# The recurrence's output products in two phases: all with states, then all with values

## The chip, the cores and the metric

The kernel runs on one core of a Trainium2 chip. What counts is the device time of one launch in microseconds, from the first to the last instruction of the program. Three runs of the kernel before the change gave 1718.55, 1724.16 and 1728.1 us, so the median is 1724.16 us.

The core has a matrix engine (TensorE, in the rows PE, and PEld for its loading of weights), a vector engine (VectorE, DVE), a scalar engine (ScalarE, ACT), a general one (GpSimd, POOL) and a queue that issues transfers (SyncE, SP). Each runs its own list of instructions in order and waits on the others through semaphores.

## The reference

Two blocks of a network work on 256 tokens of `x`, 1024 wide; the first block also has 256 tokens of `ctx`. Each block has two layers of a mixer and a gated feed-forward product. The change lies in the first block's mixer, which joins a Fourier mix, attention and a gated recurrence of four heads (64 keys, 64 values) that runs forward and backward over chunks of 64 tokens:

```python
def step(s, inp):                      # one chunk; s is the state, 64 x 64
    kc, vc, lf = inp[0], inp[1], inp[2]
    cum = jnp.cumsum(lf, axis=2)
    last = cum[:, :, -1:, :]
    s_new = jnp.exp(last[:, :, 0, :])[..., None] * s + \
        jnp.einsum('bhsd,bhse->bhde', kc * jnp.exp(last - cum), vc)
    if not with_out:
        return s_new, None
    qc = inp[3]
    o_inter = jnp.einsum('bhtd,bhde->bhte', qc * jnp.exp(cum), s)
    ...
    att = jnp.einsum('bhtd,bhsd,bhtsd->bhts', qc, kc, decay)
    return s_new, o_inter + jnp.einsum('bhts,bhse->bhte', att, vc)
```

The output of a chunk is thus a product of queries with the state before it (`o_inter`), for each direction, plus a product of weights inside the chunk with its values. In layer 0 both sequences (`ctx` is sequence 0, `x` is sequence 1) have an output, in layer 1 only `x`; `ctx` then only hands its state on.

## The kernel before

Large products (`gemm`, L176 to L178) take weights that arrive in float32, are split by ScalarE (L169) and VectorE (L170) into two halves, and enter TensorE as three products of the halves. The parts of a mixer are queued in the order of the table `STEPS`: `z0` and `z1` project gates, values and queries for two heads each, `h00` is the recurrence of sequence 0 and heads pair 0, `k`, `q`, `u`, `g` are further projections, `a` the attention. All engines' lists are laid down by a scheduler that mixes these parts, so small products of the recurrence stand between large ones in TensorE's list.

One call `h_(seq, fd)` treats a pair of heads, with the features of both heads on the 128 partitions. It has four parts:

- `hgrn_gates` turns gates and queries on TensorE (L1064), takes sigmoids on ScalarE, and makes the tile `xy` of keys and queries.
- `hgrn_levels` computes the weights inside chunks in six levels and a diagonal. In each level ScalarE copies halves of `xy` into `kq` (tile `hkm`, L1123 and L1124), TensorE makes eight products of 64 x 64 into two banks of the group `tr` (L1098), VectorE copies both banks under a mask (L1108) and scales `xy` in place for the next level.
- `hgrn_states` multiplies keys with values (L1163), folds the states of chunks on VectorE (L1178), and ScalarE copies them into `hsb` (L1190).
- `hgrn_out` makes the outputs in bank `o`. Tokens of even chunks fall on partitions 0 to 63, those of odd chunks on 64 to 127. For each chunk and head it issues up to two products of queries (128 rows, 64 columns) with states (L1204), and then one of weights with values (64 rows, 64 columns; L1206).

A float32 product is recorded as two passes, each with its own load of weights: 176 passes of L1204 are 88 products, 96 of L1206 are 48. There are six calls with outputs: four in layer 0 and two in layer 1. A call of sequence 1 has 16 products with states, one of sequence 0 has 12, and each has 8 with values.

Of the kernel before, what the change touches and what calls it, by code (L numbers as in the profile page):

```python
# [20 lines left out]
P = 128  # L21
# [8 lines left out]
# the order in which the parts of a first block's mixer are queued, for each layer  # L30
# [64 lines left out]
class Net:  # L95
    def __init__(self, ctx, tc, A, out, taps=None, stop=None):
# [15 lines left out]
        self.flip = 0  # L112
        self.late_bufs, self.late_rate = 8, 0.6
# [8 lines left out]
    # -- helpers ---------------------------------------------------------  # L122
# [36 lines left out]
    def copy(self, out, in_):  # L159
        """Copy on ScalarE and VectorE in turn."""  # L160
# [6 lines left out]
    def split(self, hi, lo, src):  # L167
        """src = hi + lo, both float32r."""
# [15 lines left out]
    # -- constants -------------------------------------------------------  # L184
    def setup(self, fp):
# [7 lines left out]
        # layer 0's c and c_ctx, and its modulation's biases, as columns  # L193
# [12 lines left out]
        # c and c_ctx as the first two of 32 columns, the others zero  # L206
# [5 lines left out]
        # sums of the rows 0, 32, 64, 96 and of 1, 33, 65, 97  # L212
# [7 lines left out]
    def setup_late(self):  # L220
        """The second block's condition and gains, as columns."""
# [30 lines left out]
    def ada_first(self, pool, k0, kn, mods):  # L252
        """k-tiles k0..k0+kn of layer 0's first scales and shifts, for c and c_ctx."""
# [22 lines left out]
    def ada_cols(self, row, j, k0, kn, dests):  # L276
        """The sums of rows as columns, k-tiles k0..k0+kn, with their biases."""
# [124 lines left out]
    def mod_tiles(self, name, gates=True):  # L402
        """Columns sh_a, sc_a, sh_f, sc_f and gate rows a, f of one modulation."""
# [13 lines left out]
    def fold_gain(self, mods, i, gi):  # L417
        """(1 + sc) *= gain, on columns."""
# [13 lines left out]
    def row_rstd(self, x, junk):  # L432
        """(mean of squares + eps) ** -0.5 of each row of x [P, D]."""
# [12 lines left out]
    def norm_t(self, pool, res, pair, sh, sc, hT, col0):  # L446
        """Two token tiles of res, normalised, modulated and turned: hT[:, :, col0 : col0 + 256]."""
# [30 lines left out]
    def norm_row(self, res, tt, sh, sc, hT, gain=None):  # L478
        """One token tile of res, normalised, modulated and turned; the turning is left pending.
        With gain, a norm with that gain goes before, and is kept in res."""  # L480
# [17 lines left out]
        else:  # L498
            # of x * gain / rms(x), in terms of x * gain
# [54 lines left out]
    def norm_first(self, pool, srcs, sh, sc, hT):  # L554
        """Two sequences from DRAM, normalised and turned while their modulations come."""
# [58 lines left out]
    def more_weights(self, name=None):  # L614
        """Open, or close, a second pool that every other chunk of weights goes to."""
# [19 lines left out]
    def gemm_steps(self, xT, ktiles, w, w0, n0, nw, toks, widths=None, after=None, ahead=0, halved=False, early=False):  # L635
        """gemm, with pauses between chunks of weights but the last ones."""
# [101 lines left out]
    def out_proj(self, xT, nk, w, w0, toks, targets, gates, after=None):  # L738
        """targets += gates * (x @ w), for the tokens at toks; after: called as each is done."""
# [43 lines left out]
    def ffn(self, pool, hT, wg, wu, wd, toks, targets, gates, parts, after=None):  # L783
        """after: called when a pair of token tiles is done."""
# [480 lines left out]
    def mix1(self, hp, pool, l, hT, start=None, late=None):  # L1265
# [81 lines left out]
        def H_(seq):  # L1347
# [4 lines left out]
            for both in levels:  # L1352
                pass
# [480 lines left out]
```

## Time and profile before

| | before |
|---|---|
| timed runs, us | 1718.55, 1724.16, 1728.1 (median 1724.16) |
| profiled execution, span in us | 1727.1 |
| TensorE busy | 1659.6 us, 96% of the span |
| VectorE, ScalarE busy | 1223.2 us (71%), 850.5 us (49%) |
| TensorE share of the chain that ended last | 72% |
| mean granted clock of TensorE | 0.989 of full speed |

The page gives the profiled execution's span and no separate time around it; it stands 2.9 us above the median and inside the three runs. Busy times of TensorE are pipelined: an instruction's duration has the tail of its pass in it, so how fast passes follow each other is read from their starts in the timeline.

### The profile page before, as it was taken

The numbers are of one execution on the slowest core, as the hardware profiler recorded it, in microseconds if no ns is written. First come the engines' busy times: TensorE is split into PE (matmuls) and PEld (weight loads), VectorE is DVE, ScalarE is ACT, GpSimd is POOL, SyncE is SP. The second block draws the span as 40 slices with busy tenths as digits, with TensorE's granted clock in tenths as the row PEclk, the third lists the DMA queues.
The fourth block names the chain that finished last, engine by engine and source line by source line (L and its number), as shares of the span: only waits on it lengthen the run. The fifth ranks groups of instructions, "written<-read, shape, count | busy, mean of one in ns | idle before, by whom it ended". The sixth has DMA issues, their size and how long they took to land.

```text
span 1727.1 us, 25168 instructions
## 1 busy us (share of the span) xinstructions
PE 1659.6 (96%) x9299; PEld 1328.1 (77%) x9299; DVE 1223.2 (71%) x2042; ACT 850.5 (49%) x1661; POOL 43.6 (3%) x53
## 2 busy tenths in 40 slices
PE   8999999999999999998999999999999999999998
PEld 5677766877777877787767878777777888778886
DVE  4556774886978887777768887787776567575555
ACT  4434483543333334554655445676544456464443
POOL 0000100000000000101000000000000000000000
PEclk9998999999999999999999999999999999999999
DMA  9550405465678886531348897543876543265653
GB/s 326 174 172 25 156 13 194 149 199 166 202 246 280 269 264 210 164 108 50 107 159 284 286 318 250 160 123 121 257 241 194 179 146 90 74 180 166 197 168 118
DMA packets 169473, 310.34 MB, mean 180 GB/s; under 512 B 12163, under 2 KB 72819, under 8 KB 169350
## 3 DMA queue, kind: packets, MB, share of 16 engines
q1 hardware_dynamic: 168966, 308.17, 55.7%
q8 instruction: 73, 1.20, 0.3%
q10 hardware_dynamic: 384, 0.56, 0.1%
q14 instruction: 50, 0.41, 0.1%
HBM read 307.64 MB, written 1.05 MB: 179 GB/s over the span
## 4 chain that ended last, share of the span: by engine, by line
PE 72%; DVE 10%; DMA 8%; ACT 5%; issue 3%; POOL 1%; SPq 1%; ACTq 0%; POOLq 0%; DVEq 0%
PE bank L178 19%; PE bank L177 19%; PE bank L176 18%; DVE wlo L170 3%; ACT whi L169 2%; PE bank L935 2%; PE bank L862 2%; DMA raw<-w_down 1%; DVE acc L357 1%; DMA adaw<-ada_w 1%; PE bank L1204 1%; DMA raw<-ffn_w_in 1%; PE bank L1431 1%; DMA raw<-ffn_w_out 1%; PE bank L320 1%
## 5 line engine op out<-in xcount | busy, mean ns | idle before, releaser
L169 ACT CAST whi<-raw 128x1024 fp32r<-128x1024 f32 (+2 forms) x420 | 400.8, 958 | 521.2 <-PE bank L178 238.1
L170 DVE TENSOR_TENSOR wlo<-raw,whi 128x1024 fp32r<-128x1024 f32 (+2 forms) x420 | 463.5, 1109 | 251.9 <-ACT whi L169 244.2
L176 PE MATMUL bank<-whi,hh 128*128 128x512 f32 (+2 forms) x1200 | 443.9, 373 | 9.3 <-ACT hh L169 5.8
L177 PE MATMUL bank<-wlo,hh 128*128 128x512 f32 (+2 forms) x1200 | 443.4, 370 | 2.7 <-DVE wlo L170 2.7
L178 PE MATMUL bank<-whi,hl 128*128 128x512 f32 (+2 forms) x1200 | 443.1, 371 | 0.2 <-DVE hl L170 0.2
L176 PEld LDWEIGHTS bank<-whi,hh 128*128 128x128 f32 x1200 | 227.8, 191 | 47.5 <-ACT hh L169 7.8
L178 PEld LDWEIGHTS bank<-whi,hl 128*128 128x128 f32 x1200 | 228.8, 191 | 36.0 <-DVE hl L170 3.6
L177 PEld LDWEIGHTS bank<-wlo,hh 128*128 128x128 f32 x1200 | 228.8, 191 | 35.8 <-DVE wlo L170 4.9
L357 DVE SCALAR_TENSOR_TENSOR acc<-adaw,cs,acc 128x1024 f32<-128x1024 f32 x154 | 196.1, 1280 | 20.1 <-DMA adaw<-ada_w 10.9
L177 PE MATMUL bank<-wlo,acth 128*128 128x512 f32 x440 | 175.0, 398 | 0.5 <-DVE wlo L170 0.5
L176 PE MATMUL bank<-whi,acth 128*128 128x512 f32 x440 | 175.3, 399 | 0.0
L178 PE MATMUL bank<-whi,actl 128*128 128x512 f32 x440 | 173.9, 395 | 0.0
L176 PE MATMUL bank<-hh,whi 128*128 128x512 f32 (+1 forms) x376 | 143.3, 382 | 0.0
L177 PE MATMUL bank<-hl,whi 128*128 128x512 f32 (+1 forms) x376 | 143.0, 381 | 0.0
L178 PE MATMUL bank<-hh,wlo 128*128 128x512 f32 (+1 forms) x376 | 142.5, 382 | 0.2 <-DVE wlo L170 0.2
L177 PEld LDWEIGHTS bank<-wlo,acth 128*128 128x128 f32 x440 | 83.5, 190 | 18.8 <-DVE wlo L170 1.1
L178 PEld LDWEIGHTS bank<-whi,actl 128*128 128x128 f32 x440 | 83.5, 190 | 18.6
L176 PEld LDWEIGHTS bank<-whi,acth 128*128 128x128 f32 x440 | 83.4, 189 | 18.5
L178 PEld LDWEIGHTS bank<-hh,wlo 128*128 128x128 f32 x376 | 70.1, 188 | 15.2 <-DVE wlo L170 0.4
L177 PEld LDWEIGHTS bank<-hl,whi 128*128 128x128 f32 x376 | 70.6, 188 | 14.5
L176 PEld LDWEIGHTS bank<-hh,whi 128*128 128x128 f32 x376 | 70.5, 188 | 14.4
L735 DVE TENSOR_TENSOR rtmp<-bank,gate 128x512 f32<-128x512 f32 x68 | 46.5, 686 | 31.5 <-PE bank L178 31.5
(295 smaller groups left out, 1904.3 us busy)
## 6 DMA issues: line engine op xcount, KB each, us to landing
adaw<-ada_w SPq DMA_DIRECT2D x96, 512.0 KB
adaw<-w_ada SPq DMA_DIRECT2D x80, 512.0 KB
raw<-ffn_w_in SPq DMA_DIRECT2D x64, 512.0 KB
raw<-w_down SPq DMA_DIRECT2D x46, 512.0 KB
raw<-ffn_w_out SPq DMA_DIRECT2D x40, 512.0 KB
raw<-w_gate SPq DMA_DIRECT2D x32, 512.0 KB
raw<-w_up SPq DMA_DIRECT2D x32, 512.0 KB
raw<-w_in SPq DMA_DIRECT2D x56, 256.0 KB
```

The source lines that it names most:

```text
L169: a = self.nc.scalar.copy(hi, src)
L170: b = self.nc.vector.tensor_sub(lo, src, hi.bitcast(F32))
L176: mm(out, lh, rh, start=start, stop=False)
L177: mm(out, lh, rl, start=False, stop=False)
L178: mm(out, ll, rh, start=False, stop=stop)
L320: nc.tensor.matmul(ps[h][32 * g : 32 * g + 32], self.cs32[:, k0 + g], raws[g][:, h * 512 : h * 512 + 512], start=k0 == 0, stop=k0 > 0,)
L357: nc.vector.scalar_tensor_tensor(acc, raw, s, acc, op0=ALU.mult, op1=ALU.add)
L735: nc.vector.tensor_mul(tmp[:, :nw], ps[:, :nw], gate[:, n0 : n0 + nw])
L862: self.nc.tensor.transpose(ps[:, i * P : i * P + P], ps_in[:, i * P : i * P + P], self.ident)
L935: self.nc.tensor.matmul(o[e * 64 : e * 64 + 64], v, pt[:, e::2, i], start=i == 0, stop=i == len(vs) - 1)
L1204: mm(dst, q, sb[:, d, i, hp], start=n == 0, stop=False)
L1431: nc.tensor.matmul(dst, q, ksT[:, i, kv, :nk], start=i == 0, stop=i == 1)
```

## The change

`hgrn_out` no longer finishes one chunk and head after the other. First it issues all products with states, so that chunks, and with them the halves of the output's partitions, alternate from product to product; then all products with values. Only the first product into each half of the bank has the flag that starts an accumulation. In the same edit the parts before it are written for a list of head pairs (`nf` of them); the table `STEPS` still calls each with one pair, so `nf` is 1 everywhere. With one pair this remains different:

- queries are turned after both halves of the gates and into a bank of their own, and copied once instead of twice; one VectorE product with a broadcast operand becomes two;
- a level's eight products alternate between the two heads, so both banks are filled at once, and the second ScalarE copy of a level becomes two;
- the products of keys with values run over chunks innermost.

```diff
     def hgrn_out(...):
-        for c in range(4):
-            r = slice((c % 2) * 64, (c % 2) * 64 + 64)
-            steps = [(d, c if d == 0 else 3 - c) for d in range(2)]
-            steps = [(d, i) for d, i in steps if 4 * seq + i]
-            for hp in range(2):
-                o0 = ((c // 2) * 4 + 2 * fd + hp) * 64
-                dst = o[r, o0 : o0 + 64]
-                for n, (d, i) in enumerate(steps):
-                    q = xy[:, 2 - d, c * 64 : c * 64 + 64]
-                    mm(dst, q, sb[:, d, i, hp], start=n == 0, stop=False)
-                v = zn[fd][r, 2 * seq + c // 2, 256 + hp * 64 : 256 + hp * 64 + 64]
-                mm(dst, att[r, hp, c // 2], v, start=False, stop=True)
+        mm, nf = self.nc.tensor.matmul, len(fds)
+        col = lambda c, fd, hp: ((c // 2) * 4 + 2 * fd + hp) * 64
+        cleared = [False, False]
+        for j, fd in enumerate(fds):
+            for d in range(2):
+                for hp in range(2):
+                    for c in range(4):
+                        i = c if d == 0 else 3 - c
+                        if 4 * seq + i == 0:
+                            continue
+                        r, o0 = slice((c % 2) * 64, (c % 2) * 64 + 64), col(c, fd, hp)
+                        q = xy[:, (2 - d) * nf + j, c * 64 : c * 64 + 64]
+                        mm(
+                            o[r, o0 : o0 + 64], q, sbs[fd][:, d, i, hp],
+                            start=not cleared[c % 2], stop=False,
+                        )
+                        cleared[c % 2] = True
+        for j, fd in enumerate(fds):
+            for hp in range(2):
+                for c in range(4):
+                    r, o0 = slice((c % 2) * 64, (c % 2) * 64 + 64), col(c, fd, hp)
+                    v = zn[fd][r, 2 * seq + c // 2, 256 + hp * 64 : 256 + hp * 64 + 64]
+                    mm(
+                        o[r, o0 : o0 + 64], att[r, hp, 2 * j + c // 2], v,
+                        start=False, stop=j == nf - 1 and hp == 1 and c > 1,
+                    )
...
     def hgrn_gates(...):
-            for j, c in enumerate((0, 1, 3) if with_q else (0, 1)):
-                nc.tensor.transpose(
-                    ps[:, j * P : j * P + P], z[:, c * P : c * P + P], self.ident
-                )
...
-                nc.vector.tensor_copy(q[:, 0, ts], ps[:, 256:384])
+        if with_q:
+            ps = self.tr_bank()
...
+            nc.vector.tensor_copy(
+                q[:, :nf], ps[:, : nf * 256].rearrange("p (j t) -> p j t", t=256)
+            )
...
     def hgrn_levels(...):
-            for hp in range(2):
-                ps = self.tr_bank()[:, :128].rearrange("p (g t) -> p g t", g=2)
-                hs = slice(hp * 64, hp * 64 + 64)
+            banks = [
+                self.tr_bank()[:, : nf * 128].rearrange("p (g t) -> p g t", t=64) for _ in range(2)
+            ]
+            for j in range(nf):
                 for c in range(4):
...
+                    for hp in range(2):
...
-                nc.scalar.copy(kv[:, ::-1, :, 1], half(xy)[:, 2:4, :, 1])
+                for s in range(2):
+                    nc.scalar.copy(
+                        kv[:, (1 - s) * nf : (2 - s) * nf, :, 1],
+                        half(xy)[:, (2 + s) * nf : (3 + s) * nf, :, 1],
+                    )
```

What moves on the engines is seen at three places. The first is TensorE's list in layer 0 where the outputs of sequence 1, head pair 0, are made; `hsb` marks products with states, `hatt` those with values, L176 to L178 large products around them. Before:

```order
L177 MATMUL bank_381_2005<-wlo_2083,hh_112 128x512
L1204 MATMUL bank_314_1603<-hsb_581,hxy_1606 64x64 x2
L1206 MATMUL bank_314_1603<-zn_586,hatt_1625 64x64
L178 MATMUL bank_381_2005<-whi_2082,hl_113 128x512
L1204 MATMUL bank_314_1603<-hsb_581,hxy_1606 64x64 x2
L1206 MATMUL bank_314_1603<-zn_586,hatt_1625 64x64
```

The last two rows then repeat until eight such pairs are through. Now, at the same place (the lines have moved by one for L176 to L178; L1249 is the product with states, L1259 that with values, L1081 the turning of queries of the next call):

```order
L177 MATMUL bank_385_2033<-whi_2110,hh_112 128x512
L1249 MATMUL bank_316_1617<-hsb_581,hxy_1620 64x64 x4
L178 MATMUL bank_385_2033<-wlo_2111,hh_112 128x512
L1249 MATMUL bank_316_1617<-hsb_581,hxy_1620 64x64 x12
L1259 MATMUL bank_316_1617<-zn_586,hatt_1640 64x64 x8
L1081 MATMUL bank_355_1837<-ident_73,zn_798 128x128 x2
```

The sixteen changes between the two shapes of a call have become two, and a large product that stood between the parts stands between the first four and the last twelve products with states.

The second place is one level of the next call in TensorE's list (`hkm` is the copy of keys and queries). Before:

```order
L177 MATMUL bank_382_2006<-wlo_2071,hh_112 128x512
L1098 MATMUL bank_357_1839<-hkm_1836 64x64 x4
L1098 MATMUL bank_358_1845<-hkm_1836 64x64 x4
L178 MATMUL bank_382_2006<-whi_2070,hl_113 128x512
L176 MATMUL bank_382_2006<-whi_2070,hh_112 128x512
```

Now, with the products of a level on line L1122:

```order
L178 MATMUL bank_386_2034<-wlo_2111,hh_112 128x512
L1122 MATMUL bank_361_1862<-hkm_1858 64x64
L1122 MATMUL bank_362_1863<-hkm_1858 64x64
L1122 MATMUL bank_361_1862<-hkm_1858 64x64
L1122 MATMUL bank_362_1863<-hkm_1858 64x64
L1122 MATMUL bank_361_1862<-hkm_1858 64x64
```

The eight products stay together between two large ones, and the banks, one for each head, now alternate.

The third place is ScalarE's list in the first call of layer 0, where the copies of two levels follow each other. Before:

```order
L1123 COPY hkm_666<-hxy_616 128x128x2
L1124 COPY hkm_666<-hxy_616 128x2x64x2
L169 CAST whi_844<-raw_841 128x1024
L1123 COPY hkm_684<-hxy_616 128x64x4
L1124 COPY hkm_684<-hxy_616 128x2x32x4
```

Now (L1150 is the first copy of a level, L1152 the two others, L170 the split of weights):

```order
L1150 COPY hkm_668<-hxy_616 128x128x2
L1152 COPY hkm_668<-hxy_616 128x64x2 x2
L170 CAST whi_851<-raw_848 128x1024
L1150 COPY hkm_687<-hxy_616 128x64x4
L1152 COPY hkm_687<-hxy_616 128x32x4 x2
```

Each level has one more copy, in place of the second; the casts of weights keep their places among them.

## Rows read from the trace of the kernel before

**Rows 1.** The page: the span, then each engine's busy time, share and instructions.

```profile
span 1727.1 us, 25168 instructions
PE 1659.6 (96%) x9299; PEld 1328.1 (77%) x9299; DVE 1223.2 (71%) x2042; ACT 850.5 (49%) x1661; POOL 43.6 (3%) x53
```

**Rows 2.** Chain of waits, 169 to 176 us (start us, us, what).

```profile
172.57 0.38 PE bank L1204 x4
172.94 0.26 PE bank L1206 x2
173.20 0.43 PE bank L176
```

**Rows 3.** PE's groups by line: busy us, mean ns of one, idle before, releaser.

```profile
L1204 PE MATMUL bank<-hsb,hxy 128*64 128x64 f32 x176 | 21.9, 244 | 0.0
...
L1098 PE MATMUL bank<-hkm 64*64 64x64 f32 x576 | 18.7, 236 | 6.1 <-ACT hkm L1124 5.8 <-DVE hatt L1106 0.3
L320 PE MATMUL bank<-adaw,cs 128*32 128x512 f32 x96 | 16.8, 599 | 0.0
L1206 PE MATMUL bank<-zn,hatt 64*64 64x64 f32 x96 | 16.5, 255 | 0.0
L1036 PE MATMUL bank<-dft,uf 128*128 128x512 f32 x24 | 12.2, 597 | 0.4 <-DVE qsT L165 0.4
```

**Rows 4.** PE's timeline, 118 to 128 us (start us, us, engine, line, operation).

```profile
120.19 0.33 PE L1204 MATMUL bank<-hsb,hxy 128*64 128x64 f32 x2
120.45 0.33 PE L1206 MATMUL bank<-zn,hatt 64*64 64x64 f32 x2
...
122.74 0.74 PE L1163 MATMUL bank<-zn,hkn 64*64 64x64 f32 x32
123.41 0.33 PE L1204 MATMUL bank<-hsb,hxy 128*64 128x64 f32 x2
...
125.58 0.38 PE L177 MATMUL bank<-wlo,hh 128*128 128x256 f32 x1
```

**Rows 5.** PE's timeline, 169.3 to 176 us.

```profile
173.47 0.39 PE L177 MATMUL bank<-wlo,hh 128*128 128x512 f32 x1
173.79 0.47 PE L1098 MATMUL bank<-hq 64*64 64x64 f32 x16
174.19 0.50 PE L178 MATMUL bank<-whi,hl 128*128 128x512 f32 x1
```

**Rows 6.** PE's timeline, 127 to 142 us.

```profile
128.43 0.33 PE L1204 MATMUL bank<-hsb,hxy 128*64 128x64 f32 x2
...
128.95 1.05 PE L281 MATMUL bank<-pick,rtmp 128*128 128x2 f32 x8
...
130.16 0.33 PE L1204 MATMUL bank<-hsb,hxy 128*64 128x64 f32 x2
...
136.15 0.58 PE L178 MATMUL bank<-whi,hl 128*128 128x256 f32 x1
```

**Rows 7.** Stretches: length, busy us of PE, PEld, DVE, ACT, POOL, clock, DMA.

```profile
136.00:141.00 5.00, 5.00 (x24) 4.88 (x24) 1.60 (x7) 1.14 (x3) 0.79 (x2) 0.50 0.00 0
...
180.00:190.00 10.00, 10.00 (x123) 7.90 (x122) 9.74 (x29) 4.99 (x11) 3.27 (x2) 1.00 0.35 107
...
806.00:812.00 6.00, 4.37 (x46) 3.00 (x50) 4.94 (x13) 1.60 (x4) 0.00 (x0) 0.57 0.16 46
```

**Rows 8.** ACT's groups by line and form: busy us, mean ns, idle before, releaser.

```profile
L1123 ACT COPY hkm<-hxy 128x256 f32<-128x256 f32 x36 | 14.9, 413 | 15.3 <-DVE hxy L1137 8.7 <-DVE hxy L1081 5.2 <-PE bank L1098 1.3
...
L1190 ACT COPY hsb<-hst 64x512 f32<-64x512 f32 x8 | 4.9, 618 | 5.8 <-DVE hst L1178 5.7
```

**Rows 9.** Timeline of all engines, layer 1, 798.9 to 819.5 us.

```profile
799.29 0.27 ACT L163 COPY v<-bank 128x128 f32<-128x128 f32 x1 [0.26 <-DVE hxh L981]
...
805.05 0.48 PE L1098 MATMUL bank<-hkm 64*64 64x64 f32 x16 [1.35 <-ACT hkm L1124]
...
818.07 1.26 ACT L1190 COPY hsb<-hst 64x512 f32<-64x512 f32 x2 [0.56 <-DVE hst L1178]
```

More of the change, by code (lines that the diff above doesn't have):

```diff
@@ new lines, in hgrn_gates @@
+            nc.scalar.activation(
+                ends[:, :, :, ts], g.rearrange("p (d j) t -> p d j t", d=2), AF.Sigmoid, scale=-1.0
+            )
+        if with_q:
+            ps = self.tr_bank()
+            for j, fd in enumerate(fds):
+                for i in range(2):
+                    o = (2 * j + i) * P
+                    nc.tensor.transpose(
+                        ps[:, o : o + P], zn[fd][:, 2 * seq + i, 3 * P : 4 * P], self.ident
+                    )
+            nc.vector.tensor_copy(
+                q[:, :nf], ps[:, : nf * 256].rearrange("p (j t) -> p j t", t=256)
+            )
@@ L1084, in hgrn_gates, with hgrn_levels @@
+        if with_q:
+            nc.vector.tensor_add(q[:, nf:], xy[:, :nf], xy[:, 3 * nf :])
+            for s in (1, 2):
+                nc.vector.tensor_mul(
+                    xy[:, s * nf : s * nf + nf], q[:, :nf], f[:, (2 - s) * nf : (3 - s) * nf]
+                )
         return f, xy, q
-    def hgrn_levels(self, pool, f, xy, q):
+    def hgrn_levels(self, pool, f, xy, q, nf):
         nc = self.nc
-        lev = self.t(pool, [P, 2, 252], F32, "hlev")
-        att = self.t(pool, [P, 2, 2, 64], F32, "hatt") if q is not None else None
+        lev = self.t(pool, [P, 2 * nf, 252], F32, "hlev", bufs=self.hbufs)
+        att = None
+        if q is not None:
+            att = self.t(pool, [P, 2, nf * 2, 64], F32, "hatt", bufs=self.hbufs)
@@ L1105, in weights @@
+            for hp, ps in enumerate(banks):
                 if mi == 6:
@@ L1147, in hgrn_states @@
-    def hgrn_states(self, pool, xy, last, zn, seq, fd, st, sb):
-        nc = self.nc
-        kn = self.t(pool, [P, 2, 2, P], F32, "hkn", bufs=1)
-        ps = self.tr_bank()
-        for d in range(2):
-            for i in range(2):
-                o = (2 * d + i) * P
-                nc.tensor.transpose(ps[:, o : o + P], xy[:, 3 * d, i * P : i * P + P], self.ident)
-        self.copy(kn, ps.rearrange("p (d i c) -> p d i c", d=2, i=2))
-        us = [self.tr_bank()[:, :256].rearrange("p (d t e) -> p d t e", d=2, t=2) for _ in range(2)]
-        for c in range(4):
-            r = slice((c % 2) * 64, (c % 2) * 64 + 64)
+        return att, cur
@@ new lines, in hgrn_states @@
+    def hgrn_states(self, pool, xy, last, zn, seq, fds, sts, sbs):
+        nc, nf = self.nc, len(fds)
+        for j, fd in enumerate(fds):
+            kn = self.t(pool, [P, 2, 2, P], F32, "hkn", bufs=1)
+            ps = self.tr_bank()
+            for d in range(2):
+                for i in range(2):
+                    o = (2 * d + i) * P
+                    nc.tensor.transpose(
+                        ps[:, o : o + P], xy[:, 3 * d * nf + j, i * P : i * P + P], self.ident
+                    )
+            self.copy(kn, ps.rearrange("p (d i c) -> p d i c", d=2, i=2))
+            us = [
+                self.tr_bank()[:, :256].rearrange("p (d t e) -> p d t e", d=2, t=2)
+                for _ in range(2)
+            ]
@@ new lines, in hgrn_states @@
+            st = sts[fd]
+            for i in range(4):
+                for d in range(2):
+                    c = i if d == 0 else 3 - i
+                    step = 4 * seq + i
+                    uu = us[c % 2][:, d, c // 2]
+                    if step == 0:
+                        nc.vector.tensor_copy(st[:, d, 0], uu)
+                    elif step < 7:
+                        nc.vector.scalar_tensor_tensor(
+                            st[:, d, step],
+                            st[:, d, step - 1],
+                            last[:, d * nf + j, c : c + 1],
+                            uu,
+                            op0=ALU.mult,
+                            op1=ALU.add,
+                        )
@@ new lines, in hgrn_states, with hgrn_out @@
+        if sbs is not None:
+            s0 = 4 * seq + (seq == 0)
+            for fd in fds:
+                for hp in range(2):
+                    hs = slice(hp * 64, hp * 64 + 64)
+                    nc.scalar.copy(
+                        sbs[fd][hs, :, s0 - 4 * seq :, hp], sts[fd][hs, :, s0 - 1 : 4 * seq + 3]
+                    )
+    def hgrn_out(self, o, xy, att, zn, seq, fds, sbs):
+        mm, nf = self.nc.tensor.matmul, len(fds)
+        col = lambda c, fd, hp: ((c // 2) * 4 + 2 * fd + hp) * 64
+        cleared = [False, False]
+        for j, fd in enumerate(fds):
+            for d in range(2):
+                for hp in range(2):
[8 more added lines that the diff above has]
+                            start=not cleared[c % 2], stop=False,
+                        )
+                        cleared[c % 2] = True
+        for j, fd in enumerate(fds):
+            for hp in range(2):
+                for c in range(4):
+                    r, o0 = slice((c % 2) * 64, (c % 2) * 64 + 64), col(c, fd, hp)
[3 more added lines that the diff above has]
+                        start=False, stop=j == nf - 1 and hp == 1 and c > 1,
+                    )
@@ L1331, in h_ @@
                 obank(seq)
-            f, xy, q = self.hgrn_gates(hg, zn, seq, fd, l, with_q)
-            *_, (att, last) = self.hgrn_levels(hg, f, xy, q)
-            self.hgrn_states(hg, xy, last, zn, seq, fd, states[fd], sbs[fd] if with_q else None)
+            xy, att = fwd(seq, (fd,))
             if not with_q:
@@ L1342, in h_, with fwd @@
                         xy, att = kept.pop((seq, d))
-                        self.hgrn_out(o, xy, att, zn, seq, d, sbs[d])
+                        self.hgrn_out(o, xy, att, zn, seq, (d,), sbs)
                 if fd == 1:
                     nc.scalar.copy(osb[seq], o)
-        def H_(seq):
-            with_q = seq in seqs
-            o = obank(seq)
-            gates = [self.hgrn_gates(hg, zn, seq, fd, l, with_q) for fd in range(2)]
-            levels = zip(*(self.hgrn_levels(hg, *g) for g in gates))
-            for both in levels:
-                pass
-            for fd, ((f, xy, q), (att, last)) in enumerate(zip(gates, both)):
-                self.hgrn_states(
-                    hg, xy, last, zn, seq, fd, states[fd], sbs[fd] if with_q else None
-                )
-            if with_q:
-                prev = None
-                for fd, ((f, xy, q), (att, last)) in enumerate(zip(gates, both)):
-                    with ExitStack() as order:
-                        if prev is not None:
-                            order.enter_context(self.tc.issue_after(prev))
-                        self.hgrn_out(o, xy, att, zn, seq, fd, sbs[fd])
-                    prev = nc.cur_bb.bb.instructions[-1]
+        def fwd(seq, fds):
+            with_q = seq in seqs
+            f, xy, q = self.hgrn_gates(hg, zn, seq, fds, l, with_q)
+            att, last = self.hgrn_levels(hg, f, xy, q, len(fds))
+            self.hgrn_states(hg, xy, last, zn, seq, fds, states, sbs if with_q else None)
+            return xy, att
+        def H_(seq):
+            xy, att = fwd(seq, (0, 1))
+            if seq in seqs:
+                o = obank(seq)
+                self.hgrn_out(o, xy, att, zn, seq, (0, 1), sbs)
                 nc.scalar.copy(osb[seq], o)
```

114 lines of the change are left out of this document (49 added, 65 removed).

## The prediction

> **What bounds the kernel now.** I read the page first: TensorE is busy for 1659.6 of 1727.1 us [rows 1], so time taken from its list is time taken from the span wherever nothing else is about to be late. I then asked the chain of waits for the stretch in which a call of sequence 1 makes its outputs. The chain runs through nothing but these products: 0.38 us for four passes of L1204, 0.26 us for two passes of L1206, and so on until the next large product at 173.20 us [rows 2]. The same holds at the other five calls: L1204 and L1206 never have idle time before them [rows 3], so TensorE issues them as fast as it can, and they stand on the path that sets the end.
>
> What they cost is read from starts. Two passes take 0.26 us [rows 4], four 0.38 us, so a further pass of the same shape costs (0.38 - 0.26) / 2 = 0.06 us, and the change of shape that each block begins with 0.26 - 0.12 = 0.14 us [rows 2]. A call of sequence 1 is eight times 0.38 + 0.26 = 5.1 us. The first call of sequence 0 takes 2.55 us up to 122.74 and 2.17 us from 123.41 to 125.58, together 4.7 us [rows 4]; the second takes 0.52 us and then, from 130.16 to 136.15, 5.99 us, together 6.5 us [rows 6]. All six: 4 x 5.1 + 4.7 + 6.5 = 31.6 us.
>
> **The change part by part.**
>
> *Outputs.* The number of passes stays. A call of sequence 1 now has two changes of shape instead of sixteen. Its 32 passes with states alternate between the column halves of the array. If the halves work beside each other, the pace is half a pass, 0.03 us; if not, 0.06 us. The nearest rows say beside each other. L1098 puts its products alternately on two column halves and issues 16 passes in 0.40 us [rows 5], 0.025 us each with the change of shape in it, less than half of 0.06. L320, whose loads cover all 128 rows as L1204's do, goes in turn over four column groups: 16.8 us for 96 passes of 512 columns, 0.18 us each, against 12.2 / 24 = 0.51 us for L1036, which has as many columns and no groups [rows 3]. The 16 passes with values alternate too, between the lower rows with the lower columns and the upper with the upper. So a call of sequence 1 becomes 32 x 0.03 + 0.14 + 16 x 0.03 + 0.14 = 1.7 us, one of sequence 0, with 24 passes, 1.5 us. Six calls: 4 x 1.7 + 2 x 1.5 = 9.8 us. That removes 31.6 - 9.8 = 21.8 us. The other bound, no overlap at all, is 32 x 0.06 + 16 x 0.06 + 0.28 = 3.2 us and 2.7 us: 18.2 us, and 13.4 us removed. I take the first, as L1098 is the nearest row.
>
> The Trainium skill has a sentence against this change ("TensorE: Matmul & The Clock Gate", Part 3: Packing small matmuls — row/col tiling): "LDWEIGHTS overlaps with in-flight MATMULs only when row_grp differs". All products with states use all rows, so by that rule their loads would not hide and the sum would be near the bound without overlap, 13.4 us removed. The trace disagrees as far as it goes: within one head L1098 keeps the same 64 rows for eight passes, and 0.025 us a pass leaves no room for exposed loads [rows 5].
>
> A second rule, in "TensorEngine Tiling (Array Packing)", Gotcha 1: PSUM Pressure, says that different row tiles cannot access one PSUM bank at the same time. The products with values alternate between row tiles and write one bank; no run here shows that yet. By the rule they would keep 0.06 us a pass, 6 x 16 x 0.03 = 2.9 us less gain.
>
> *Clock.* In the second call of sequence 0 the granted clock falls, and it stays at 0.50 of full speed, the 1.2 GHz level, through 136 to 141 us while large products already run [rows 7]; before it fell, TensorE had a few large products, L281's tiny ones and outputs in blocks of two and four passes [rows 6]. At the 2.4 GHz level that stretch from 136.15 would take half, 2.4 us less. With the call at 1.5 us the thin stretch is shorter by 5 us; I count 2 us, with 0 and 2.4 as ends.
>
> *Levels.* Each level keeps its 16 passes and its one change of shape, so 0.40 us [rows 5] can fall only as far as four tiles at once allow, 4 x 0.06 + 0.14 = 0.38 us. There are 42 such groups: 0.02 x 42 = 0.8 us less. L1163, which already mixes four tiles, takes 0.67 us for 32 passes [rows 4], about the same pace per pass; I count 0.8, from 0 to 1. On ScalarE one copy of 413 ns [rows 8] becomes two of half the size, 0.27 us each by the nearest copy [rows 9]: 0.13 us more in each of 36 levels, 4.7 us of an engine that is busy 49%. The large products between two levels hide it in most places. It is exposed where TensorE waits for the copy: 5.8 us of idle time before L1098 in all [rows 3], of which one wait of 1.35 us in layer 1 [rows 9]. These waits fall on the first call of layer 0 and the last of layer 1, 12 levels: 12 x 0.13 = 1.6 us more, from 0 to 4.7. That both banks are now full only at the end of a level delays the first of VectorE's two masked copies by half a level, 0.2 us; the scaling of `xy` needs not these copies, so I count nothing, at most 0.2 x 12 = 2.4 us where cover is gone.
>
> *Queries.* Per call one VectorE copy goes and one product comes, of the same elements in all: nothing, between 0.5 us either way. The turning into a third bank is one more small group in TensorE's list, at most one start of 0.14 us: 6 x 0.1 = 0.6 us more, from 0 to 0.8.
>
> *New wait.* Before, the second head's first product with a state came after a product with values, a block later; now it comes 8 passes, 0.24 us, after the first head's. ScalarE's two copies of states take 618 ns each [rows 8, 9], one per head. Where outputs follow directly on the states, in three of six calls, TensorE can wait up to 0.62 - 0.24 = 0.4 us, with large products queued behind: 1.2 us more, from 0 (a large product laid between, as at the places shown) to 1.2.
>
> Sum: -21.8 - 2.0 - 0.8 + 1.6 + 0.6 + 1.2 = -21.2 us. On the profiled span, 1727.1 - 21.2 = 1705.9 us; that execution stood 2.9 us above the median, so I predict 1724.2 - 21.2 = **1703 us**, a gain of 1.2%. The loading of weights behind the outputs keeps up: ScalarE and the transfers are far from full in layer 0's mixer [rows 7], and what follows a mixer starts from TensorE's last products. Adding the ends one way (-21.8 - 2.4 - 1) gives 1699 us, the other way (-13.4 + 4.7 + 2.4 + 0.5 + 0.8 + 1.2) 1720 us.
>
> **Rivals.**
>
> *The halves do not work beside each other.* Then the change does only half of what it says, and takes out changes of shape alone: 13.4 us instead of 21.8, so -12.8 us, 1711 us. For it: no row has full-height, 64-column loads alternating. Against it: L1098 and L320. Chance 0.13.
>
> *VectorE takes the place.* In 180 to 190 us it is busy 9.74 of 10 us [rows 7]. If the stretches after the four calls of sequence 1 are bound by it, their gain (4 x 3.4 = 13.6 us) stays as waiting before L1122 and the large products: -7.6 us, 1717 us. Against it: the outputs themselves leave it idle, since the chain stays on TensorE [rows 2]. Chance 0.12.
>
> *TensorE is held in front of the levels: slower.* A level's eight products now stand together behind three copies and need two free banks, and TensorE's list cannot pass them. The price is the waiting before L1122, now 5.8 / 36 = 0.16 us a level. In layer 1 one wait was 1.35 us [rows 9], and in that stretch the clock was granted at 0.57 [rows 7]. If all 36 levels waited 1 us more, that is 36 - 21.2 = 15 us slower, 1739 us. It decides from 21.2 / 36 = 0.6 us a level more; from 0.83 us the kernel is measurably slower. For it: the third copy and the bank pair. Against it: large products stand between levels in the list. Chance 0.06.
>
> **How the numbers follow.** Forecast 0.69, rivals 0.13, 0.12 and 0.06. What a measurement can tell from no change is 0.5%, 8.6 us. Faster by more: all but a little of the forecast (0.67), most of the first rival (0.10) and a third of the second (0.04): 0.81. Within it: 0.13. Slower: the third, 0.06. The range reaches from 1695, a little below the favourable end for the spread of the runs shown, to 1719, nearly the unfavourable one; it takes in the first two rivals and leaves out the third.
>
> **What would show it.** In the profile after, L1249 must follow in starts of about 0.03 us a pass: 32 passes in 1 us, and L1259's 16 in half of one; 0.06 us means the first rival for the states, or the bank rule for the values. The whole call should take 1.7 us, and the clock should stay up around 130 us. Idle time before L1122 should stay below 8 us; 25 us or more there would be the third rival. VectorE's share behind the calls and its waits on TensorE tell the second. I am wrong if the outputs shrink and the span does not follow.

## The result and the profile after

| | before | changed |
|---|---|---|
| median of the timed runs, us | 1726.13 (4 runs, 1718.55 to 1728.99) | 1705.44 (4 runs, 1704.73 to 1707.19) |
| ratio, 95% interval | | 0.9882 [0.9865, 0.9900] |
| profiled span, us | 1727.1 | 1703.0 |

The change makes the kernel 20.7 us faster, 1.2%. The median of before has one run more than the three shown ahead of the prediction.

The page of the changed kernel gives the span and busy times that answer to [rows 1]:

```profile
span 1703.0 us, 25231 instructions
...
PE 1637.8 (96%) x9299; PEld 1313.0 (77%) x9299; DVE 1221.2 (72%) x2042; ACT 854.0 (50%) x1697; POOL 44.7 (3%) x53
```

TensorE makes the same 9299 passes, in 21.8 us less. The span fell by 24.1 us. ScalarE has 36 instructions more, the third copy of each level.

TensorE's groups by line in the changed kernel (columns as in [rows 3]):

```profile
L1122 PE MATMUL bank<-hkm 64*64 64x64 f32 x576 | 18.1, 235 | 2.6 <-ACT hkm L1152 2.1 <-DVE hatt L1133 0.5
...
L1249 PE MATMUL bank<-hsb,hxy 128*64 128x64 f32 x176 | 8.1, 229 | 0.8 <-ACT hsb L1230 0.8
L1259 PE MATMUL bank<-zn,hatt 64*64 64x64 f32 x96 | 5.1, 241 | 0.0
```

The two output lines are busy for 13.2 us, where they were for 21.9 + 16.5 = 38.4 us [rows 3]. The idle time before the levels' products fell from 6.1 to 2.6 us. New is 0.8 us of waiting before L1249.

The pace is read from starts, as the prediction did. TensorE's timeline of the changed kernel, where sequence 1, head pair 1 of layer 0 makes its outputs with no other product between:

```profile
177.23 1.15 PE L1249 MATMUL bank<-hsb,hxy 128*64 128x64 f32 x32
178.31 0.68 PE L1259 MATMUL bank<-zn,hatt 64*64 64x64 f32 x16
178.93 0.66 PE L1004 MATMUL bank<-ident,qnat 128*128 128x128 f32 x4
```

With 0.14 us for the change of shape, 32 passes with states take 178.31 - 177.23 = 1.08 us, 0.029 us each, and 16 with values 0.62 us, 0.030 us each. The call takes 1.70 us, as forecast. The others, by their starts too, took 1.61 us (2.01 us less the 0.40 us of a level laid into it) and 2.19 us (sequence 0) and 1.84 us in layer 0, about 2.3 and 1.85 us in layer 1; other products split these five into two to four pieces. All six: 11.5 us, against 9.8 us forecast.

The one of 2.19 us ran partly at a lower clock. Windows of the changed kernel (columns as in [rows 7]):

```profile
124.00:128.00 4.00, 4.00 (x51) 3.79 (x49) 1.48 (x10) 1.30 (x3) 0.44 (x1) 1.00 0.47 135
128.00:132.00 4.00, 4.00 (x37) 3.78 (x34) 1.82 (x8) 1.52 (x4) 0.99 (x2) 0.57 0.00 0
132.00:136.00 4.00, 4.00 (x28) 3.22 (x26) 3.01 (x6) 3.69 (x9) 0.70 (x1) 1.00 0.11 11
136.00:140.00 4.00, 4.00 (x35) 2.68 (x34) 3.92 (x16) 2.18 (x7) 0.00 (x0) 1.00 0.38 122
```

The dip is still there, but short. TensorE's timeline shows where it ends (a large product of this form starts every 0.12 us at the 2.4 GHz level and every 0.21 us here):

```profile
128.17 1.12 PE L1259 MATMUL bank<-zn,hatt 64*64 64x64 f32 x16
129.22 0.58 PE L177 MATMUL bank<-whi,hh 128*128 128x256 f32 x1
...
131.09 0.41 PE L179 MATMUL bank<-whi,hl 128*128 128x256 f32 x1
131.30 0.35 PE L177 MATMUL bank<-whi,hh 128*128 128x256 f32 x1
131.50 0.28 PE L178 MATMUL bank<-wlo,hh 128*128 128x256 f32 x1
```

The half clock ends at about 131.3 us; 0.57 of full speed over the 4 us of that window makes some 3.4 us of it. Before, 0.50 was granted through all of 136 to 141 us [rows 7].

Where the gain arrives is seen at two marks. L863 (L862 before) turns the weights of the attention and first starts when layer 0's mixer is done; L1037 (L1036 before) is the Fourier product, which last starts near the end of layer 1's mixer. One line of the source view each (duration min/median/max, first and last start), before:

```profile
L862 PE MATMUL bank<-ident,prob x288: 270/273/329, 215.9 to 1507.5; 128*128 128x128 f32 x144
L1036 PE MATMUL bank<-dft,uf x24: 590/592/697, 213.5 to 855.1; 128*128 128x512 f32 x24
```

and in the changed kernel:

```profile
L863 PE MATMUL bank<-ident,prob x288: 270/273/332, 201.6 to 1483.7; 128*128 128x128 f32 x144
L1037 PE MATMUL bank<-dft,uf x24: 590/592/697, 199.2 to 833.5; 128*128 128x512 f32 x24
```

The attention starts 14.3 us earlier. The four calls of layer 0 shrank from 4.7 + 6.5 + 2 x 5.1 = 21.4 to 7.3 us, 14.1 us less. The last Fourier pass of layer 1 starts at 833.5 instead of 855.1 us, 21.6 us earlier. From there the program took 872.0 us before and 869.5 now. That difference does not go with the change: five of the kernels below took 869.5 to 870.1 us, one of them with the old outputs, but the changed kernel run again took 872.2 and the one with one copy fewer 874.4. So 21.6 of the 24.1 us belong to the stretch that was changed, and the other 2.5 us are no more than executions differ by.

### The profile page after: what moved, and what is told of

It reads as the page before. It is cut to its first block, busy times and chain, and to the rows that moved or that the text cites. A ratio compares the mean times of both kernels' runs of the same rounds, so it can differ in the third digit from the quotient of the medians.

```text
span 1703.0 us, 25231 instructions
## 1 busy us (share of the span) xinstructions
PE 1637.8 (96%) x9299; PEld 1313.0 (77%) x9299; DVE 1221.2 (72%) x2042; ACT 854.0 (50%) x1697; POOL 44.7 (3%) x53
## 3 DMA queue, kind: packets, MB, share of 16 engines
HBM read 307.64 MB, written 1.05 MB: 181 GB/s over the span
## 4 chain that ended last, share of the span: by engine, by line
PE 71%; DVE 10%; DMA 9%; ACT 5%; issue 3%; POOL 1%; SPq 0%; POOLq 0%; ACTq 0%; DVEq 0%
PE bank L179 19%; PE bank L177 19%; PE bank L178 19%; DVE wlo L171 3%; ACT whi L170 2%; PE bank L936 2%; DMA raw<-w_up 2%; PE bank L863 2%; DVE acc L358 1%; DMA adaw<-w_ada 1%; DMA raw<-w_gate 1%; PE bank L1478 1%; PE bank L321 1%; PE bank L1004 1%; ACT colj L387 1%
## 5 line engine op out<-in xcount | busy, mean ns | idle before, releaser
L170 ACT CAST whi<-raw 128x1024 fp32r<-128x1024 f32 (+2 forms) x420 | 400.5, 959 | 521.7 <-PE bank L179 239.7
L178 PE MATMUL bank<-wlo,hh 128*128 128x512 f32 (+2 forms) x1200 | 443.5, 370 | 2.1 <-DVE wlo L171 2.1
L178 PEld LDWEIGHTS bank<-wlo,hh 128*128 128x128 f32 x1200 | 229.0, 191 | 33.8 <-DVE wlo L171 3.2
L358 DVE SCALAR_TENSOR_TENSOR acc<-adaw,cs,acc 128x1024 f32<-128x1024 f32 x154 | 196.0, 1279 | 18.1 <-DMA adaw<-w_ada 8.8
L178 PE MATMUL bank<-wlo,acth 128*128 128x512 f32 x440 | 174.5, 397 | 0.5 <-DVE wlo L171 0.5
L178 PE MATMUL bank<-hl,whi 128*128 128x512 f32 (+1 forms) x376 | 143.0, 381 | 0.0
L178 PEld LDWEIGHTS bank<-wlo,acth 128*128 128x128 f32 x440 | 83.2, 189 | 18.5 <-DVE wlo L171 0.9
L178 PEld LDWEIGHTS bank<-hl,whi 128*128 128x128 f32 x376 | 70.6, 188 | 14.4
```

The source lines that it names most:

```text
L170: a = self.nc.scalar.copy(hi, src)
L178: mm(out, lh, rl, start=False, stop=False)
L358: nc.vector.scalar_tensor_tensor(acc, raw, s, acc, op0=ALU.mult, op1=ALU.add)
```

## The experiments

Seven runs were made, one of them of the changed kernel again, each timed beside the kernel before. The first four shared the runs of before on one chip (median 1725.39 us), the last three on another (1725.8 us).

### The outputs alone, and the rest alone

The first puts only the new `hgrn_out` into the kernel before:

```diff
-        for c in range(4):
-            ...
-            for hp in range(2):
-                ... (states, then values, per chunk and head)
+        for d in range(2):
+            for hp in range(2):
+                for c in range(4):
+                    ... (products with states)
+        for hp in range(2):
+            for c in range(4):
+                ... (products with values)
```

> The kernel before with the two-phase outputs alone; gates, levels and states as they were. Theory (the gain is all in the output products: two changes of shape in place of sixteen, and two column halves beside each other): 21.8 us of products go, and none of the side edits' costs come (about 1.4 us), so some 22 us faster than before, about 1704 us; a call of sequence 1 takes 1.7 to 1.9 us, passes follow at 0.03 us. Rival (the side edits, above all the levels' products alternating between heads, carry a third or more of it): no more than 14 us faster, about 1712 us.

The second keeps every other edit and puts the old loop back:

```diff
-        for j, fd in enumerate(fds):
-            for d in range(2):
-                ...
+        for c in range(4):
+            steps = [(d, c if d == 0 else 3 - c) for d in range(2)]
+            for hp in range(2):
+                for n, (d, i) in enumerate(steps):
+                    mm(dst, q, sbs[fd][:, d, i, hp], start=n == 0, stop=False)
+                mm(dst, att[r, hp, c // 2], v, start=False, stop=True)
```

> The changed kernel with the old outputs, chunk by chunk and head by head; all side edits stay. Theory: within 3 us of the kernel before, on the slow side if at all (one more copy in 36 levels, 0.8 us less on TensorE): about 1727 us. Rival (side edits carry the gain): 7 us faster or more, 1719 us or less.

Measured: the outputs alone 1704.81 us, ratio 0.9891 [0.9871, 0.9912]; the rest alone 1724.69 us, ratio 1.0003 [0.9988, 1.0018]. In the timed runs the two-phase outputs carry the whole gain: 20.6 us, where the rival allowed 14. The other edits are worth nothing that can be measured, between 2 us less and 3 us more by the interval. In the first run's profile the calls of sequence 1 in layer 0 take 1.84 and 1.85 us by their starts, within the 1.7 to 1.9 us expected. Groups of the kernel with the outputs alone:

```profile
L1098 PE MATMUL bank<-hkm 64*64 64x64 f32 x576 | 19.0, 239 | 5.0 <-ACT hkm L1124 4.7 <-DVE hatt L1106 0.3
...
L1205 PE MATMUL bank<-hsb,hxy 128*64 128x64 f32 x176 | 8.0, 229 | 0.0
L1214 PE MATMUL bank<-zn,hatt 64*64 64x64 f32 x96 | 4.4, 225 | 0.0
```

and of the kernel with the rest alone:

```profile
L1248 PE MATMUL bank<-hsb,hxy 128*64 128x64 f32 x176 | 22.3, 247 | 0.8 <-ACT hsb L1230 0.8
L1122 PE MATMUL bank<-hkm 64*64 64x64 f32 x576 | 18.0, 233 | 2.3 <-ACT hkm L1152 1.9 <-DVE hatt L1133 0.5
L1250 PE MATMUL bank<-zn,hatt 64*64 64x64 f32 x96 | 16.6, 257 | 0.0
```

The output lines cost 38.9 us in the old order and 12.4 us in the new one, whatever stands around them. The shorter waiting before the levels (2.3 instead of 5.0 us) and the new 0.8 us before the states go with the other edits. At the mark of the last Fourier pass the other edits stand 2.8 us ahead with the old outputs (852.3 against 855.1 us) and 3.7 us with the new ones (833.5 against 837.2). These are single executions, and the timed runs do not show it.

This pair also tells of the clock. Windows of the kernel with the rest alone:

```profile
128.00:132.00 4.00, 4.00 (x29) 3.25 (x28) 1.81 (x11) 0.90 (x3) 1.40 (x2) 0.76 0.18 68
132.00:136.00 4.00, 4.00 (x25) 3.06 (x24) 0.50 (x3) 0.00 (x0) 0.00 (x0) 0.50 0.00 0
136.00:140.00 4.00, 4.00 (x20) 3.77 (x20) 0.44 (x2) 0.86 (x2) 0.00 (x0) 0.50 0.00 0
```

and of the kernel with the outputs alone:

```profile
128.00:132.00 4.00, 4.00 (x46) 3.93 (x45) 1.79 (x8) 1.99 (x5) 0.70 (x1) 1.00 0.00 0
132.00:136.00 4.00, 3.98 (x25) 3.04 (x24) 3.49 (x7) 3.18 (x8) 0.70 (x1) 1.00 0.22 62
```

The long stretch at half clock goes with the old outputs, although the profile shows TensorE busy for all of it: the two kernels with them have about 10 us of it between 128 and 142 us, the seven runs without them 3.4 us or none from 124 to 144 us. Whether it is the changes of shape or the length of the calls that brings it was not tested.

### The column halves one after the other

Two phases, and so two changes of shape, but all products into the lower column half (output partitions 0 to 63) before those into the upper:

```diff
-            for d in range(2):
-                for hp in range(2):
-                    for c in range(4):
+            for half in range(2):
+                for d, hp in ((0, 0), (0, 1), (1, 0), (1, 1)):
+                    for c in (half, half + 2):
...
-            for hp in range(2):
-                for c in range(4):
+            for half in range(2):
+                for hp, c in ((0, half), (0, half + 2), (1, half), (1, half + 2)):
```

> The changed kernel, still two phases with two changes of shape, but each phase does all products of one column half and then all of the other, so that no two neighbours are on different halves. Theory (half of the pace comes from halves working beside each other): passes follow at 0.055 to 0.06 us in place of 0.03, 48 passes x 0.03 = 1.4 us more for each of four calls and 40 x 0.03 = 1.2 us for two, 8 us slower than the changed kernel, about 1713 us, still 12 to 13 us faster than before. Rival (full-height loads never overlap, the gain came from the changes of shape): the same as the changed kernel, about 1705 us, with the same pace of passes as there.

Measured: 1708.34 us, ratio 0.9903 [0.9887, 0.9918]. TensorE's timeline at the call shown above:

```profile
178.25 1.90 PE L1249 MATMUL bank<-hsb,hxy 128*64 128x64 f32 x32
180.08 0.96 PE L1259 MATMUL bank<-zn,hatt 64*64 64x64 f32 x16
180.97 0.66 PE L1004 MATMUL bank<-ident,qnat 128*128 128x128 f32 x4
```

With halves apart a pass with states takes (1.83 - 0.14) / 32 = 0.053 us instead of 0.029, one with values (0.89 - 0.14) / 16 = 0.047 instead of 0.030, and the call 2.72 us instead of 1.70. So alternating halves do work beside each other; the rival of one pace is refuted by the starts. By these paces a call of sequence 0 takes 2.72 - 8 x 0.053 = 2.30 us, and the six calls 4 x 2.72 + 2 x 2.30 = 15.5 us: of the 31.6 us before, 16 go without any overlap and 6 more with it. In the 16 are some 1.8 us of clock, since the second call of sequence 0 ran mostly at the 1.2 GHz level before (6.5 against 4.7 us for the first). The flags that start an accumulation are those of the changed kernel here, and the pace in one half is still near the 0.06 us of before, so the flags are not what changed it.

The time alone does not show this: 1708.34 us is 2.6 to 2.9 us above the changed kernel's 1705.44 and 1705.70, and the intervals overlap. My 8 us was too large. I had 0.06 us a pass, half the difference of two rows (0.38 and 0.26 us), where it is 0.053; and this execution had no dip of the clock at 128 to 136 us, which the changed kernel's had.

### Four blocks in a call

Alternating halves, but each call in four blocks of states and values, eight changes of shape in place of two:

```diff
-            for d in range(2):
-                for hp in range(2):
-                    for c in range(4):
+        for pair in range(2):
+            for hp in range(2):
+                for d in range(2):
+                    for c in (2 * pair, 2 * pair + 1):
                         ... (products with states)
-            for hp in range(2):
-                for c in range(4):
+                for c in (2 * pair, 2 * pair + 1):
                     ... (products with values)
```

> The changed kernel with alternating halves, but outputs in four blocks (a pair of chunks and a head each): eight products or fewer with states, then two with values, so eight changes of shape a call in place of two. Theory (a change of shape costs 0.14 us): 6 x 0.14 = 0.8 us a call, six calls, 5 us slower than the changed kernel, about 1710 us. Rival (a change of shape costs only where one half is refilled alone; with both halves in turn it is hidden): within 1.5 us of the changed kernel, about 1706 us.

Measured: 1708.50 us, ratio 0.9904 [0.9889, 0.9920]. TensorE's timeline at the same call:

```profile
178.64 0.45 PE L1250 MATMUL bank<-hsb,hxy 128*64 128x64 f32 x8
179.02 0.33 PE L1258 MATMUL bank<-zn,hatt 64*64 64x64 f32 x4
179.28 0.45 PE L1250 MATMUL bank<-hsb,hxy 128*64 128x64 f32 x8
...
181.22 0.66 PE L1004 MATMUL bank<-ident,qnat 128*128 128x128 f32 x4
```

Four times 0.38 + 0.26 us come to 2.58 us, 0.88 more than with two phases: six more changes of shape cost 0.88 / 6 = 0.147 us each, against the 0.14 us of the prediction. Over six calls that is 5.3 us; the time shows 3 us, again with overlapping intervals. The price holds by the starts; the time alone lies between the two forecasts of 1710 and 1706 us and settles nothing.

A rival to the change of shape is that a product with values waits for the one with states just before it, which writes the same place in the bank. The changed kernel speaks against it, where states follow a large product into another bank (sequence 1, head pair 0):

```profile
158.20 0.45 PE L1249 MATMUL bank<-hsb,hxy 128*64 128x64 f32 x8
158.58 0.50 PE L178 MATMUL bank<-wlo,hh 128*128 128x512 f32 x1
```

These eight passes take 0.38 us, 0.15 us more than 8 x 0.029, though no product just before them wrote there.

### The changed kernel again, and with one copy fewer

The changed kernel itself ran again beside the next two:

> The changed kernel itself, run beside the next two on one chip, so that they can be compared with it directly and with the runs of e1 to e4 through the kernel before. Both theories: a ratio of 0.988 to the kernel before, about 20 us faster.

Measured: 1705.70 us, ratio 0.9880 [0.9854, 0.9905], as before. Its clock dips too, as its windows show:

```profile
124.00:128.00 4.00, 4.00 (x53) 3.60 (x53) 1.65 (x10) 1.04 (x3) 1.44 (x2) 0.80 0.11 40
128.00:132.00 4.00, 4.00 (x29) 3.96 (x28) 1.60 (x7) 1.89 (x4) 0.70 (x1) 0.78 0.00 0
```

Counted from the start of the execution it comes earlier, but it falls on the same products. TensorE's timeline:

```profile
126.42 1.12 PE L1259 MATMUL bank<-zn,hatt 64*64 64x64 f32 x16
127.47 0.58 PE L177 MATMUL bank<-whi,hh 128*128 128x256 f32 x1
...
129.56 0.39 PE L177 MATMUL bank<-whi,hh 128*128 128x256 f32 x1
129.77 0.29 PE L178 MATMUL bank<-wlo,hh 128*128 128x256 f32 x1
```

The values of the second call of sequence 0 take 1.05 us again, and the large products behind them start every 0.21 us up to 129.6 us, all 1.7 us earlier than in the first execution, since the whole list ran that much ahead (the call shown above starts at 175.52 instead of 177.23 us). So both executions of this program have the dip at the same place and some 3.4 us long. The kernel with four blocks has one of that length too; those with the outputs alone, with the halves apart and with one copy fewer have none at this call. What decides it is not shown.

The next takes back the third ScalarE copy of a level:

```diff
-                for s in range(2):
-                    nc.scalar.copy(
-                        kv[:, (1 - s) * nf : (2 - s) * nf, :, 1],
-                        half(xy)[:, (2 + s) * nf : (3 + s) * nf, :, 1],
-                    )
+                nc.scalar.copy(kv[:, ::-1, :, 1], half(xy)[:, 2:4, :, 1])
```

> The changed kernel with the second ScalarE copy of a level as one instruction again (36 copies fewer). Theory (the extra copy is hidden but in the 12 levels where TensorE waits for it): 1.6 us faster than the changed kernel, 0 to 3 us. Rival (the copy is on the path of every level): 4.7 us faster or more, 36 x 0.13 us.

Measured: 1707.45 us, ratio 0.9901 [0.9876, 0.9926], so no gain against 1705.70. ScalarE's groups of the changed kernel:

```profile
L1152 ACT COPY hkm<-hxy 128x128 f32<-128x128 f32 x72 | 18.8, 300 | 7.2 <-DVE hxy L1169 6.9
```

and of the one with a copy fewer:

```profile
L1152 ACT COPY hkm<-hxy 128x256 f32<-128x256 f32 x36 | 14.9, 413 | 7.5 <-DVE hxy L1166 7.2 <-DVE hxy L1100 0.2
```

ScalarE saves 3.9 us, but TensorE's idle time before the levels is 3.2 us here and 2.6 us with the third copy. The times cannot tell 1.6 us from nothing; the idle time shows none of it, so the copy looks hidden where I had counted 1.6 us exposed.

### Both head pairs in one call

The lists of head pairs allow one call for both (`H0`, `H1`). It halves the number of small groups, but puts a sequence's levels behind both projections; its tiles have one buffer instead of two (`hbufs`):

```diff
-    "z0 h00 z1 g h01 e k h10 h11 q u m a r",
-    "z0 h00 h10 z1 e h01 k h11 q g u m a r",
+    "z0 z1 g H0 e k H1 q u m a r",
+    "z0 z1 e H0 k H1 q g u m a r",
...
-        self.hbufs = 2
+        self.hbufs = 1
```

> The changed kernel with its recurrence called for both pairs of heads at once (the steps of a sequence become one, queued after both projections of gates; tiles of the recurrence once instead of twice). Theory (what the outputs showed holds for the levels: changes of shape cost TensorE 0.14 us each): 21 groups of levels' products instead of 42 and 3 output calls instead of 6 save (21 + 6) x 0.14 = 4 us, if the chain of levels stays covered, so about 1701 us. Rival (the recurrence now starts later and in one piece, and its chain through VectorE and ScalarE lies open): 5 us slower than the changed kernel or more, with idle time of TensorE before the levels' products of 10 us or more.

Measured: 1706.60 us, ratio 0.9899 [0.9877, 0.9921], no different from the changed kernel. Its groups:

```profile
L1122 PE MATMUL bank<-hkm 64*64 64x64 f32 x576 | 14.7, 237 | 5.6 <-ACT hkm L1152 4.6 <-DVE hatt L1131 0.8
...
L1249 PE MATMUL bank<-hsb,hxy 128*64 128x64 f32 x176 | 8.0, 229 | 0.0
L1259 PE MATMUL bank<-zn,hatt 64*64 64x64 f32 x96 | 3.4, 221 | 0.0
```

The levels' products take 3.4 us less, the waiting before them 3.0 us more. Layer 0's attention starts at 196.5 us instead of 201.6, but from there to the last Fourier pass of layer 1 it takes 638.2 us instead of 631.9: 2.4 us more up to the end of layer 0's feed-forward product (700.3 against 703.0 us) and 3.9 us more behind it. So the 5 us are given back. Neither my 4 us nor the rival's loss came. No version tried is measurably better than the changed kernel.

## Why the prediction was right

The forecast was 21.2 us less; 20.7 were measured. The distance of 1703 to 1705.44 us is mostly that of the two medians of before, 1724.16 and 1726.13.

- **Outputs**, forecast -21.8 us, the favourable bound: 31.6 - 11.5 = 20 us by starts, the whole gain as far as the timed runs tell. The pace of L1098 was the right neighbour to lean on. The missing 1.7 us are the dip of the clock in one call (0.4 us) and the pieces into which other products cut five of the calls.
- **What the two parts of it weigh** I had as 13.4 us for fewer changes of shape and 8.4 us for the overlap. It is nearer 16 and 6, since a pass without overlap takes 0.047 to 0.053 us. The first of the two holds in both counts some 1.8 us that are the clock's and not the shape's: the 5.99 us of the prediction were read mostly at half clock.
- **Clock**, forecast -2 us: in the profiled executions the half clock outside the outputs cost 136.15 to about 141.2 us before, so 2.5 us, and about 1.0 us after 129.22 us now. The gain of some 1.5 us was within its ends, but "the clock should stay up around 130 us" held only in some programs. A dip stayed in both executions of the changed kernel, at the same products.
- **Levels**, forecast -0.8 us: L1122 is busy 18.1 us instead of 18.7, a gain of 0.6; by starts a group of 16 takes 0.39 to 0.40 us, where it took 0.40 to 0.41.
- **Third copy**, forecast +1.6 us: this is the term that was mis-sized. A half copy was recorded with 300 ns, not 270, but two of them overlap: the line is busy 3.9 us longer than with one copy, where I had counted 4.7. On TensorE none of it is seen. I had taken all 12 levels of two calls as waiting for a copy. The trace of before has such a wait at six levels, 5.8 us in all, and the changed kernel at three, 2.1 us in all. The long one, 1.35 us before, is still there (the timeline of layer 1 in the changed kernel):

```profile
788.18 0.70 PE L1122 MATMUL bank<-hkm 64*64 64x64 f32 x16 [1.34 <-ACT hkm L1152]
```

One exposed level says nothing of the others; the 0.8 us that are left for all 35 leave no room for 1.6.

- **Waiting before the levels** had no term of its own: it fell by 3.5 us, from 6.1 to 2.6. It goes with the other edits, as the pair of experiments showed. Part of it is waited elsewhere: up to the last Fourier pass TensorE's idle time fell by 2.0 us in all.
- **Queries**, forecast +0.6 us: not measured apart. It lies within the -2 to +3 us of all other edits.
- **New wait**, forecast +1.2 us in three calls: there is one, of 0.76 us, in one call. The timeline of all engines in the changed kernel, layer 1:

```profile
798.64 0.74 PE L1201 MATMUL bank<-zn,hkn 64*64 64x64 f32 x32
...
801.07 1.23 DVE L1217 SCALAR_TENSOR_TENSOR hst<-hst,hlev,bank 128x64 f32<-128x64 f32 x6
...
802.39 1.26 ACT L1230 COPY hsb<-hst 64x512 f32<-64x512 f32 x2 [1.46 <-DVE hst L1217]
803.06 0.45 PE L1249 MATMUL bank<-hsb,hxy 128*64 128x64 f32 x8 [0.76 <-ACT hsb L1230]
```

TensorE waits for the first of the two copies, not for the second, because VectorE folds the states (L1217) 1.7 us after their products are through: its list has two products of the query norm and a split of weights in between. The second copy is covered, since the scheduler laid large products between the first 8 passes and the other 24.

That the sum came within 0.5 us is partly luck: outputs, clock and levels gave some 2.5 us less than forecast, and copy and new wait cost some 2 us less.

**The rivals.** *The halves do not work beside each other*: refuted by 0.029 against 0.053 us. *VectorE takes the place*: in 160 to 170 us of the changed kernel it is busy 9.61 of 10 us, and still the attention behind that mixer starts 14.3 us earlier, with 14.1 us of outputs removed. *TensorE held in front of the levels*: the waiting there is 2.6 us, not 25 or more. The window of the changed kernel behind its third call:

```profile
160.00:170.00 10.00, 10.00 (x139) 6.75 (x137) 9.61 (x35) 6.36 (x20) 1.65 (x2) 1.00 0.01 2
```

**The two rules cited ahead.** The rule that loads overlap with products only when the row group differs (the Trainium skill, "TensorE: Matmul & The Clock Gate", Part 3: Packing small matmuls — row/col tiling) would give one pace for both orders of the states, which all use 128 rows. The runs gave 0.029 and 0.053 us, so the measurement decides against it here. The rule that row tiles cannot share a bank (the Trainium skill, "TensorEngine Tiling (Array Packing)", Gotcha 1: PSUM Pressure) would have kept the values at their old pace. They write one bank from alternating row tiles at 0.030 us a pass, and at 0.047 us in one half, so no such cost is seen here.

What stays open: the two experiments on the outputs lose about 5 us by starts and 3 us in time. At the last Fourier pass they stand at 836.5 (halves apart) and 838.4 us (four blocks), against 833.5 and 831.8 us in the two executions of the changed kernel, 3 to 7 us behind, each a single execution, which fits the starts. For the halves apart 1.0 us of the difference is the dip of the clock behind the values, which it did not have; the kernel with four blocks had a dip as long as the changed kernel's. The rest is within the intervals.

## What to carry to other kernels

Small products are read from their starts: the first pass after a change of tile shape and the pass that follows on the same shape have different prices, and two rows with different counts give both. Where a list changes shape every few passes, grouping by shape comes first; alternating the column halves then nearly halves the time of a pass again. A wait is counted at each place where the trace has it, and not for every level that looks alike.

## What the runs showed of the hardware

- A change of tile shape costs 0.14 to 0.15 us in these float32 products, as much as five alternating passes.
- Products of full height and 64 columns, alternating between column halves, follow each other in 0.029 us, those in one half in 0.053 us.
- TensorE's clock can fall to the 1.2 GHz level while the profile shows TensorE busy all the time: with outputs in blocks of two and four passes 0.50 was granted through 132 to 140 us, in the runs with longer blocks for some 3.4 us or not at all. Two executions of the changed kernel had the dip at the same products.
